# Nine fast product groups a layer instead of eight, and the residual parked in DRAM to make room

## The chip, the cores and the metric

The kernel runs on one core of a Trainium2 chip. The metric is device microseconds of one execution; times of runs are medians. The engines named below: TensorE (PE) multiplies, and PEld is its weight load; VectorE (DVE) and ScalarE (ACT) do the elementwise work; SyncE (SP) issues the DMAs; GpSimd (POOL) does nothing here.

## The reference

Two layers on x of 256 positions by 2048 features, all in float32. Layer 0 has a recurrent block (RG-LRU), layer 1 sliding-window attention with sinks; each ends with the same feed forward network, which is the part that the change touches.

```python
D_MODEL, SEQ, DEPTH = 2048, 256, 2
D_FF = 5632

def swiglu_ffn(x, g, w_in, w_out):
    h = rms_norm(x, g)
    gate, up = jnp.split(h @ w_in, 2, axis=-1)
    return x + (jax.nn.silu(gate) * up) @ w_out

for layer in range(DEPTH):
    if layer < N_REC:
        x = recurrent_block(x, ...)
    else:
        if layer == N_REC:
            k_band, v_band = shared_kv(x, kv_norm_g, w_kv, k_norm_g)
        x = attn_block(x, ..., k_band, v_band)
    x = swiglu_ffn(x, norm2_g[layer], ffn_w_in[layer], ffn_w_out[layer])
```

## The kernel before

**Layout.** Features lie on the 128 partitions, positions (T = 256) along the free dimension. The residual x is four tiles of 128 x 1024, each with four blocks of 128 features. Every weight is streamed once from DRAM, in jobs of 256 rows x 512 columns (512 KB, one DMA on SP's queue).

**Precision.** Each float32 operand is split into a high part `hi` (rounded to fp32r) and the rest `lo`, and a product is made of three matmuls: hi·hi, hi·lo and lo·hi. ACT makes `hi` (line 337), DVE subtracts to get `lo` (line 338).

**Jobs.** `stream` goes through a list of jobs. At job i it asks for the load of job i+4, splits the weights of job i+3, and emits the matmuls of job i. There are four buffers each of raw, hi and lo. Background work (generators) is emitted in between as far as a budget of DVE and ACT time allows (`DVE_TICK`, `ACT_TICK`, `DEBT`). That gives the order of the program. The framework then plans from it the order on each engine: an instruction whose inputs are ready in its model may go ahead of earlier ones that are not, and `issue_after` and `keep_in_program_order` restrain that.

**Feed forward input.** The 2 x 5632 columns are 22 groups of 512, each of eight jobs. A group yields 256 gate and 256 up features, and `silu(gate) * up` goes to a raw hidden tile.

- Groups 0 to 3 (`PLAIN`) start before the norm is known: they multiply x times the norm's gain, and their results are scaled by 1/rms afterwards (`start`). Meanwhile `normed` prepares the scaled and split input `xn`, and for six of the eight jobs also the mixed input `mx`.
- Of the others, groups 5, 7, ... 19 (`FAST`) are fast: in six of the eight jobs (`PAIRS`) the eight block products of a job are replaced by seven, in Strassen's way (Winograd's form), with mixed inputs and mixed weights. `mix` makes the mixed weights (lines 348 to 354: 349 to 351 build them in a tile d, 352 and 354 split them, 348 and 353 split the unmixed part). A job has then 21 matmuls instead of 24 (line 543). In the jobs 0 and 4 (`EVEN`) the mixed products come first. `joined` sums the product blocks into gate and up. The result stands with positions on the partitions, so that `turn` transposes it (line 738, four transposes), deferred until job 4 of the next fast group, or job 3 of the group after the last one.
- The remaining ones, 4, 6, ... 20 and 21, are plain groups on `xn` (`direct`). The one after the last fast group, 20, has some wide products: one matmul of 512 columns with the high and low part of x side by side in place of two of 256. `self.SYNC` puts such wide products into other groups of the program as well.
- After group 20, `split` is spawned: it splits the raw hidden tiles for the output product, each pair with one ACT copy and one DVE subtraction, which must come behind the last `mix` (`self.mark`).

**Feed forward output.** Four groups of 22 jobs; after each, `residual` adds the results into one tile of x.

**Memory.** Besides fixed buffers there are 33 work tiles of 128 x 1024 (`s0` to `s32`), handed out in the order in which they came free: five "near" ones, which `mix` and `joined` ask for, and 28 others. Between them lies a gap of 64 bytes. The four tiles of x are fixed and stand beside them.

Of the kernel before, what the change touches and what calls it, by code (L numbers as in the profile page):

```python
# [12 lines left out]
F32 = mybir.dt.float32  # L13
F32R = mybir.dt.float32r
AF = mybir.ActivationFunctionType
ALU = mybir.AluOpType

P = 128
D = 2048
T = 256  # L20
# [29 lines left out]
class Trunk:  # L50
# [10 lines left out]
    DEBT = 2500.0  # L61
    SYNC = (0, 1, 2)
    PLAIN = 4
    FAST = tuple(range(5, 20, 2))
    PAIRS = (0, 1, 2, 4, 5, 6)
    EVEN = (0, 4)
    OWED = 9000.0
    NEAR = 5
    MORE = 2800.0
    WARM = 30  # L70
    DVE_TICK = 640.0
# [2 lines left out]
    def __init__(self, ctx, tc, dram):  # L74
        self.tc, self.nc, self.d = tc, tc.nc, dram
        nc = self.nc
        const = ctx.enter_context(tc.tile_pool(name="const", bufs=1))
        psum = ctx.enter_context(tc.tile_pool(name="psum", bufs=1, space=bass.MemoryType.PSUM))
        self.par = const.tile([P, NPAR], F32, name="par")
        self.con = const.tile([P, NCON], F32, name="con")  # L80
        self.cc = const.tile([P, 32], F32, name="cc")
        self.rstd = [const.tile([P, T + 2], F32, name=f"rstd{i}") for i in range(2)]
        self.nm, self.nt = (const.tile([P, T + 2], F32, name=n) for n in ("nm", "nt"))
        self.r2 = const.tile([P, 2], F32, name="r2")
        self.rrs = [const.tile([P, 48], F32, name=f"rr{i}") for i in range(2)]
        self.zero = const.tile([P, P + T], F32R, name="zero")
        const.tile([P, PAD], F32, name="pad")
        self.x = [const.tile([P, 4, T], F32, name=f"x{i}") for i in range(4)]
        self.raw = [const.tile([P, 1024], F32, name=f"raw{i}") for i in range(4)]
        self.hi = [const.tile([P, 1024], F32R, name=f"hi{i}") for i in range(4)]  # L90
        self.lo = [const.tile([P, 1024], F32R, name=f"lo{i}") for i in range(4)]
        self.tmps = deque(const.tile([P, T], F32, name=f"t{i}") for i in range(4))
        self.halves = deque(const.tile([P, T], F32, name=f"h{i}") for i in range(4))
        self.sq = deque(const.tile([P, T], F32, name=f"sq{i}") for i in range(3))
        self.acc = self.sq.popleft()
        self.whole = [deque((i, 0) for i in range(self.NEAR, 33)), deque((i, 0) for i in range(self.NEAR))]
        self.stamp = 0
        self.keep = False
        self.part = {(d, n): deque() for d in (F32, F32R) for n in (False, True)}
        self.spool = const  # L100
        for i in range(33):
            if i == self.NEAR:
                const.tile([P, 16], F32, name="step")
            const.tile([P, 4 * T], F32, tag=f"s{i}", name=f"s{i}")
        self.held = {}
        self.sets = [[psum.tile([P, 512], F32, name=f"b{4 * i + j}") for j in range(4)] for i in range(2)]
        self.banks = deque(b for q in self.sets for b in q)
        self.misc = 0
        self.started = False
        self.jobs = []  # L110
        self.mixed = {}
        self.pend = deque()
        self.bg = deque()
        self.tick = -2 * self.LD
        self.dve = 0.0
        self.act = 0.0

# [45 lines left out]
    def double(self, dt=F32R, near=False):  # L163
        i, _ = self.pool(dt, near).popleft()
        s = self.spool.tile([P, 4 * T], dt, tag=f"s{i}", name=f"s{i}")
        self.held[id(s)] = (i, s)
        return s

    def back(self, i):
        self.whole[i < self.NEAR].append((i, self.stamp))  # L170
# [431 lines left out]
    def ffn(self, l, xs, r, gains, rn, col, out=None):  # L602
# [6 lines left out]
        two = lambda ap: ap.rearrange("p (a c) -> p a c", c=T)  # L609

        def normed():
# [3 lines left out]
            for p in range(8):  # L615
                while self.spare() < 4:
                    yield 1
                n, d = self.slot(F32), self.double()
# [5 lines left out]
                v = d[:, :].rearrange("p (a b c) -> p a b c", a=2, b=2)  # L624
# [6 lines left out]
                if p in self.PAIRS:  # L631
                    c, m = self.slot(F32), self.double()
# [11 lines left out]
                    self.free(c)  # L644
                    yield
                self.free(n)

        def split():
            for p in range(NH // 2):
# [19 lines left out]
        for g in range(NH // 2):  # L669
# [25 lines left out]
            def direct(ps, g=g):  # L695
# [14 lines left out]
                raw(g, s)  # L710
                if g == self.FAST[-1] + 1:
                    self.spawn(split())

            def joined(q, g=g):
                p1, c, u, h = self.half(), self.double(F32, True), self.slot(F32, True), self.slot(F32)
                twice = lambda ap: ap.unsqueeze(1).to_broadcast([P, 2, T])
                at = lambda i, n=1: q[i // 2][:, i % 2 * T:(i % 2 + n) * T]
                self.a(p1, at(5))
                self.tt(c[:, 3 * T:4 * T], at(4), p1, ALU.add)
                self.tt(two(u), two(at(6, 2)), twice(c[:, 3 * T:4 * T]), ALU.add)  # L720
                self.tt(c[:, 3 * T:4 * T], at(7), u[:, 0:T], ALU.add)
                self.tt(c[:, 0:T], at(3), p1, ALU.add)
                self.tt(c[:, T:2 * T], at(1), u[:, 0:T], ALU.add)
                self.tt(c[:, 2 * T:3 * T], at(2), u[:, T:2 * T], ALU.add)
                self.tt(c[:, 3 * T:4 * T], at(0), c[:, 3 * T:4 * T], ALU.add)
                for p in q:
                    self.free_bank(p)
                self.a(c[:, 0:2 * T], c[:, 0:2 * T], AF.Silu)
                self.tt(h, c[:, 2 * T:4 * T], c[:, 0:2 * T], ALU.mult)
                self.free_half(p1)  # L730
                self.free(c)
                self.free(u)

                def turn():
                    p = self.mbank()
                    for j in range(2):
                        for i in range(2):
                            nc.tensor.transpose(p[:, j * T + i * P:j * T + i * P + P],  # L738
                                                h[:, i * T + j * P:i * T + j * P + P],
                                                self.con[:, K_ID:K_ID + P])  # L740
                    s = self.slot(F32)
                    self.a(s, p)
                    self.free_mbank(p)
                    self.free(h)
                    raw(g, s)
                self.pend.append(turn)
# [4 lines left out]
            elif g in self.FAST:  # L751
                self.fast_group(src, xn, mx, g, joined, g == self.FAST[-1])
            else:
                end = g == self.FAST[-1] + 1
                self.group(src, ND, xn, direct, g == NH // 2 - 1, (0, 3, 4, 5) if end else (), True, 3 if end else None)
            if g == 0:
                def begin():
                    self.spawn(normed())
                    self.DEBT = self.OWED
                    self.keep = True  # L760
                self.jobs[-8] = self.with_(self.jobs[-8], begin)
        n = len(self.jobs)
        self.project(self.d[f"ffn_out{l}"], NH, hid, gains, rn, out)

        def end():
            self.DEBT = Trunk.DEBT
            self.keep = False
        self.jobs[n] = self.with_(self.jobs[n], end)

    def with_(self, job, first):  # L770
        src, mm, fast = job
# [600 lines left out]
```

## Time and profile before

| | us |
|---|---|
| median of 3 runs | 1979.45 (1979.3 to 1979.98) |
| profiled execution | 1980.0 |
| its span, first to last instruction | 1978.2 |
| PE busy | 1969.5, 16576 matmuls |
| PEld busy | 1927.9 |
| DVE busy | 1489.9 |
| ACT busy | 1123.8 |

In layer 1, group 0 of the feed forward input starts at about 1266 us of the span, group 4 at 1355.2, the first fast group at 1377.0, and the output product at 1735.6; layer 0 has the same stages some 970 us earlier.

Times in the profile's rows are microseconds from the start of the span, durations of one instruction are nanoseconds where "mean ns" stands. Matmuls overlap in the pipeline: one lasts 276 ns, but the next starts 113 ns after it, so PE's work is read from the distance of starts, or from the chain of waits, which lists the time that each piece added. A row of a timeline is start, duration, engine, line and operation, output<-inputs, shapes, count, and in brackets the idle time ahead of it with what ended it.

### The profile page before, as it was taken

The page shows a single profiled execution, that of the slowest core. Times are in us where ns is not written, and L with a number is a line of the kernel's source. Part 1 is how long each engine was busy: PE and PEld are TensorE (multiplying, and loading weights), DVE is VectorE, ACT ScalarE, POOL GpSimd, SP SyncE. Part 2 cuts the span into 40 slices and gives each one's busy share as a digit, 9 for nine tenths or more (in the row PEclk, how much of TensorE's full clock was granted, in tenths as well). Part 3 has the DMA queues.
Part 4 walks back from the last instruction along what each step waited for, and adds up shares of the span by engine and source line. Part 5 has one row for each costly group of instructions (what it writes and reads, how often), then busy time and mean ns, then how long its engine had stood idle before and what let it go on. Part 6 is the DMA issues. An engine that isn't in the chain of part 4 may idle for free. (4 is left out here: it accounts for less than half of the span.)

```text
span 1978.2 us, 40228 instructions
## 1 busy us (share of the span) xinstructions
PE 1969.5 (100%) x16576; PEld 1927.9 (97%) x16576; DVE 1489.9 (75%) x2375; ACT 1123.8 (57%) x1642; POOL 0.2 (0%) x4
## 2 busy tenths in 40 slices
PE   9999999999999999999999999999999999999999
PEld 9999999999999999999998789999999999999999
DVE  8989868788888896554667776697888888844443
ACT  7798756555555565444556775564555555644442
POOL 0000000000000000000000000000000000000000
PEclk9999999999999999999999999999999999999999
DMA  7555655555566556556554334555666565656663
GB/s 274 189 190 180 202 195 181 197 199 196 193 207 208 199 193 202 193 191 199 195 182 145 122 118 151 191 189 185 200 209 209 193 201 196 205 196 204 204 204 128
DMA packets 105016, 376.57 MB, mean 190 GB/s; under 512 B 11648, under 2 KB 13824, under 8 KB 104832
## 3 DMA queue, kind: packets, MB, share of 16 engines
q1 hardware_dynamic: 104544, 373.60, 57.1%
q8 instruction: 129, 2.11, 0.4%
q14 instruction: 55, 0.45, 0.1%
q10 hardware_dynamic: 288, 0.40, 0.1%
HBM read 371.86 MB, written 2.10 MB: 189 GB/s over the span
## 5 line engine op out<-in xcount | busy, mean ns | idle before, releaser
L385 PE MATMUL b<-s,hi 128*128 128x256 f32 (+1 forms) x8190 | 1093.4, 280 | 2.0 <-ACT s L127 1.3
L385 PEld LDWEIGHTS b<-s,hi 128*128 128x128 f32 x8190 | 1017.8, 188 | 15.2 <-ACT s L127 2.2
L338 DVE TENSOR_TENSOR lo<-raw,hi 128x1024 fp32r<-128x1024 f32 (+1 forms) x609 | 740.7, 1220 | 374.2 <-ACT hi L337 371.3
L337 ACT ACTIVATE hi<-raw 128x1024 fp32r<-128x1024 f32 (+1 forms) x609 | 641.0, 1056 | 524.4 <-PE b L385 430.9
L385 PE MATMUL b<-s,lo 128*128 128x256 f32 x4224 | 626.7, 276 | 0.0
L385 PEld LDWEIGHTS b<-s,lo 128*128 128x128 f32 x4224 | 547.3, 188 | 0.2
L352 ACT ACTIVATE s<-s 128x1024 fp32r<-128x1024 f32 x96 | 102.1, 1063 | 169.9 <-DVE s L351 169.9
L543 PE MATMUL b<-hi,s 128*128 128x256 f32 x1088 | 180.5, 277 | 0.0
L543 PEld LDWEIGHTS b<-hi,s 128*128 128x128 f32 x1088 | 154.7, 188 | 0.0
L543 PE MATMUL b<-s,s 128*128 128x256 f32 x1152 | 149.7, 279 | 0.0
L543 PEld LDWEIGHTS b<-s,s 128*128 128x128 f32 x1152 | 139.8, 189 | 0.0
L354 DVE TENSOR_TENSOR s<-s,s 128x1024 fp32r<-128x1024 f32 x96 | 117.6, 1225 | 27.6 <-ACT s L352 27.6
L543 PE MATMUL b<-lo,s 128*128 128x256 f32 x544 | 129.5, 276 | 0.0
L127 ACT ACTIVATE s<-s 128x512 fp32r<-128x512 f32 (+3 forms) x174 | 85.2, 521 | 30.9 <-DVE s L136 23.9
L543 PEld LDWEIGHTS b<-lo,s 128*128 128x128 f32 x544 | 92.6, 188 | 0.0
L353 DVE TENSOR_TENSOR lo<-raw,hi 128x768 fp32r<-128x768 f32 x96 | 91.3, 951 | 0.0
L348 ACT ACTIVATE hi<-raw 128x768 fp32r<-128x768 f32 x96 | 78.7, 841 | 21.2 <-issue 11.7
L349 DVE TENSOR_TENSOR s<-raw 128x512 f32<-128x512 f32 x96 | 66.1, 689 | 24.2 <-DMA raw<-in_ffn_in 23.1
L1262 PE MATMUL b<-hi,s 128*128 128x512 f32 x256 | 83.4, 406 | 0.0
L136 DVE TENSOR_TENSOR s<-s,s 128x512 fp32r<-128x512 f32 (+2 forms) x143 | 74.6, 551 | 4.9 <-ACT s L127 4.7
L127 ACT ACTIVATE s<-b 128x256 fp32r<-128x256 f32 (+4 forms) x114 | 51.0, 481 | 24.6 <-PE b L1236 6.7
L1262 PEld LDWEIGHTS b<-hi,s 128*128 128x128 f32 x256 | 45.8, 188 | 9.6 <-issue 1.2
(118 smaller groups left out, 1105.9 us busy)
## 6 DMA issues: line engine op xcount, KB each, us to landing
raw<-in_ffn_in SPq DMA_DIRECT2D x352, 512.0 KB, 3.7
raw<-in_ffn_out SPq DMA_DIRECT2D x176, 512.0 KB, 3.9
raw<-in_lru_in SPq DMA_DIRECT2D x63, 512.0 KB, 4.0
raw<-in_lru_out SPq DMA_DIRECT2D x32, 512.0 KB, 3.4
raw<-in_w_q SPq DMA_DIRECT2D x32, 512.0 KB, 3.2
raw<-in_w_o SPq DMA_DIRECT2D x32, 512.0 KB, 3.3
raw<-in_gate SPq DMA_DIRECT2D x8, 512.0 KB, 4.1
raw<-in_kv SPq DMA_DIRECT2D x8, 512.0 KB, 3.3
```

The lines of the kernel that those rows point to most:

```text
L127: self.nc.scalar.activation(out, in_, func, **kw)
L136: self.nc.vector.tensor_tensor(out, a, b, op)
L337: self.nc.scalar.activation(hi[:, q], raw[:, q], AF.Copy)
L338: self.nc.vector.tensor_tensor(lo[:, q], raw[:, q], hi[:, q].bitcast(F32), ALU.subtract)
L348: act(hi[:, q], raw[:, q], AF.Copy)
L349: tt(two(d[:, 0:2 * T]), two(raw[:, T:3 * T]), raw[:, 0:T].unsqueeze(1).to_broadcast([P, 2, T]), ALU.subtract)
L352: act(mh[:, :], d[:, :], AF.Copy)
L353: tt(lo[:, q], raw[:, q], hi[:, q].bitcast(F32), ALU.subtract)
L354: self.mark = tt(ml[:, :], d[:, :], mh[:, :].bitcast(F32), ALU.subtract)
L385: self.nc.tensor.matmul(ps[f][:, 0:c1 - c0], w, x2[k][:, c0:c1], start=f not in begun, stop=last and all(q[1] != f for q in todo[n + 1:]))
L543: nc.tensor.matmul(st["ps"][b][:, h % 2 * T:(h % 2 + n) * T], x, w, start=b not in st["begun"], stop=True, skip_group_check=True)
L1262: nc.tensor.matmul(st[g][b][:, :], x, q, start=c + kt == 0 and x is xh and q is wh, stop=c == 7 and kt == 1 and q is wl)
```

## The change

In each layer's feed forward input the fast groups are 4, 6, ... 20: nine instead of eight, the first straight behind group 3. The plain group with the wide products and the spawn of `split` is then 21, the last one. To have work tiles for it, x becomes four tiles of the work pool, which has 37 now, seven of them near. As soon as `normed` has read a tile of x, `park` stores it to DRAM and frees it; in the output product `fetch` loads the four back, in the jobs 2, 7, 12 and 17 (the first 22 jobs end with the first use). `joined` sums with fewer, wider operations (512 columns where two of 256 stood next to each other), which leaves gate and up interleaved in another order, so that `turn` reads the halves the other way round, and it no longer uses near tiles. During the stage the budget per half job for DVE is 780 ns instead of 640 (740 in layer 1).

```diff
--- before.py
+++ after.py
@@ -61,11 +61,13 @@
     DEBT = 2500.0
     SYNC = (0, 1, 2)
     PLAIN = 4
-    FAST = tuple(range(5, 20, 2))
+    FAST = tuple(range(4, 21, 2))
     PAIRS = (0, 1, 2, 4, 5, 6)
     EVEN = (0, 4)
     OWED = 9000.0
-    NEAR = 5
+    BUSY = 780.0
+    WORK = 37
+    NEAR = 7
     MORE = 2800.0
     WARM = 30
     DVE_TICK = 640.0
@@ -85,7 +87,6 @@
         self.rrs = [const.tile([P, 48], F32, name=f"rr{i}") for i in range(2)]
         self.zero = const.tile([P, P + T], F32R, name="zero")
         const.tile([P, PAD], F32, name="pad")
-        self.x = [const.tile([P, 4, T], F32, name=f"x{i}") for i in range(4)]
         self.raw = [const.tile([P, 1024], F32, name=f"raw{i}") for i in range(4)]
         self.hi = [const.tile([P, 1024], F32R, name=f"hi{i}") for i in range(4)]
         self.lo = [const.tile([P, 1024], F32R, name=f"lo{i}") for i in range(4)]
@@ -93,16 +94,22 @@
         self.halves = deque(const.tile([P, T], F32, name=f"h{i}") for i in range(4))
         self.sq = deque(const.tile([P, T], F32, name=f"sq{i}") for i in range(3))
         self.acc = self.sq.popleft()
-        self.whole = [deque((i, 0) for i in range(self.NEAR, 33)), deque((i, 0) for i in range(self.NEAR))]
+        self.whole = [deque((i, 0) for i in range(self.NEAR, self.WORK)), deque((i, 0) for i in range(self.NEAR))]
         self.stamp = 0
+        self.tick = -2 * self.LD
         self.keep = False
         self.part = {(d, n): deque() for d in (F32, F32R) for n in (False, True)}
         self.spool = const
-        for i in range(33):
+        for i in range(self.WORK):
             if i == self.NEAR:
                 const.tile([P, 16], F32, name="step")
             const.tile([P, 4 * T], F32, tag=f"s{i}", name=f"s{i}")
         self.held = {}
+        self.x, self.xt = [None] * 4, [None] * 4
+        for i in range(4):
+            self.place(i)
+        self.dram = ctx.enter_context(tc.tile_pool(name="dram", bufs=1, space=bass.MemoryType.DRAM))
+        self.away = {}
         self.sets = [[psum.tile([P, 512], F32, name=f"b{4 * i + j}") for j in range(4)] for i in range(2)]
         self.banks = deque(b for q in self.sets for b in q)
         self.misc = 0
@@ -111,7 +118,6 @@
         self.mixed = {}
         self.pend = deque()
         self.bg = deque()
-        self.tick = -2 * self.LD
         self.dve = 0.0
         self.act = 0.0
 
@@ -165,6 +171,22 @@
         s = self.spool.tile([P, 4 * T], dt, tag=f"s{i}", name=f"s{i}")
         self.held[id(s)] = (i, s)
         return s
+
+    def place(self, i):
+
+        n, _ = self.whole[0].pop() if self.tick < 0 else self.whole[1].popleft()
+        s = self.spool.tile([P, 4 * T], F32, tag=f"s{n}", name=f"s{n}")
+        self.held[id(s)] = (n, s)
+        self.xt[i], self.x[i] = s, s[:, :].rearrange("p (f t) -> p f t", t=T)
+
+    def park(self, i):
+        self.away[i] = self.dram.tile([P, 4 * T], F32, name=f"away{self.tick}_{i}")
+        self.nc.sync.dma_start(self.away[i][:, :], self.xt[i][:, :])
+        self.free(self.xt[i])
+
+    def fetch(self, i):
+        self.place(i)
+        self.nc.sync.dma_start(self.xt[i][:, :], self.away[i][:, :])
 
     def back(self, i):
         self.whole[i < self.NEAR].append((i, self.stamp))
@@ -644,6 +666,8 @@
                     self.free(c)
                     yield
                 self.free(n)
+                if p % 2:
+                    self.park(p // 2)
 
         def split():
             for p in range(NH // 2):
@@ -712,22 +736,21 @@
                     self.spawn(split())
 
             def joined(q, g=g):
-                p1, c, u, h = self.half(), self.double(F32, True), self.slot(F32, True), self.slot(F32)
+                c, u, h = self.double(F32), self.double(F32), self.slot(F32)
                 twice = lambda ap: ap.unsqueeze(1).to_broadcast([P, 2, T])
                 at = lambda i, n=1: q[i // 2][:, i % 2 * T:(i % 2 + n) * T]
-                self.a(p1, at(5))
-                self.tt(c[:, 3 * T:4 * T], at(4), p1, ALU.add)
-                self.tt(two(u), two(at(6, 2)), twice(c[:, 3 * T:4 * T]), ALU.add)
-                self.tt(c[:, 3 * T:4 * T], at(7), u[:, 0:T], ALU.add)
-                self.tt(c[:, 0:T], at(3), p1, ALU.add)
-                self.tt(c[:, T:2 * T], at(1), u[:, 0:T], ALU.add)
-                self.tt(c[:, 2 * T:3 * T], at(2), u[:, T:2 * T], ALU.add)
-                self.tt(c[:, 3 * T:4 * T], at(0), c[:, 3 * T:4 * T], ALU.add)
+                part = lambda i, n=1: u[:, i * T:(i + n) * T]
+                self.a(part(3), at(5))
+                self.tt(part(0), at(4), part(3), ALU.add)
+                self.tt(two(part(1, 2)), two(at(6, 2)), twice(part(0)), ALU.add)
+                self.tt(part(0), at(7), part(1), ALU.add)
+                self.tt(c[:, 0:2 * T], at(0, 2), part(0, 2), ALU.add)
+                self.tt(c[:, 2 * T:4 * T], at(2, 2), part(2, 2), ALU.add)
                 for p in q:
                     self.free_bank(p)
-                self.a(c[:, 0:2 * T], c[:, 0:2 * T], AF.Silu)
-                self.tt(h, c[:, 2 * T:4 * T], c[:, 0:2 * T], ALU.mult)
-                self.free_half(p1)
+                v = c[:, :].rearrange("p (a b c) -> p a b c", a=2, b=2)
+                self.a(v[:, :, 1, :], v[:, :, 1, :], AF.Silu)
+                self.tt(two(h), v[:, :, 0, :], v[:, :, 1, :], ALU.mult)
                 self.free(c)
                 self.free(u)
 
@@ -736,7 +759,7 @@
                     for j in range(2):
                         for i in range(2):
                             nc.tensor.transpose(p[:, j * T + i * P:j * T + i * P + P],
-                                                h[:, i * T + j * P:i * T + j * P + P],
+                                                h[:, (1 - i) * T + j * P:(1 - i) * T + j * P + P],
                                                 self.con[:, K_ID:K_ID + P])
                     s = self.slot(F32)
                     self.a(s, p)
@@ -757,6 +780,7 @@
                 def begin():
                     self.spawn(normed())
                     self.DEBT = self.OWED
+                    self.usual, self.DVE_TICK = self.DVE_TICK, self.BUSY
                     self.keep = True
                 self.jobs[-8] = self.with_(self.jobs[-8], begin)
         n = len(self.jobs)
@@ -764,8 +788,11 @@
 
         def end():
             self.DEBT = Trunk.DEBT
+            self.DVE_TICK = self.usual
             self.keep = False
         self.jobs[n] = self.with_(self.jobs[n], end)
+        for i in range(4):
+            self.jobs[n + 2 + 5 * i] = self.with_(self.jobs[n + 2 + 5 * i], lambda i=i: self.fetch(i))
 
     def with_(self, job, first):
         src, mm, fast = job
```

## The prediction

> **What bounds the kernel now.** I read the page's busy shares first, then the chain of waits around the changed stage, then the timelines of VectorE (DVE), TensorE (PE) and ScalarE (ACT) where the first fast group of layer 1 starts.
>
> ```profile
> span 1978.2 us, 40228 instructions
> PE 1969.5 (100%) x16576; PEld 1927.9 (97%) x16576; DVE 1489.9 (75%) x2375; ACT 1123.8 (57%) x1642; POOL 0.2 (0%) x4
> 1376.99 19.90 PE b L543 x174
> 1396.89 21.76 PE b L385 x192
> 1418.65 9.96 PE b L543 x87
> 1428.61 0.44 PE b L738 x4
> 1429.05 9.96 PE b L543 x87
> ```
>
> PE is busy in all but 8.7 us of the span, so the time is the sum of PE's steps. The chain (start, duration, what) gives their prices. A plain group is 192 matmuls in 21.76 us, 113.3 ns each. A fast group is 174 matmuls (six jobs of 21, two of 24) in 2 x 9.96 = 19.92 us. The turn of an earlier fast group's result, four transposes, is a further 0.44 us, which the first fast group of a layer doesn't have.
>
> **The sum.** Each layer exchanges one plain group for a fast one: groups 5, 7 ... 19 become 4, 6 ... 20. Away go 21.76 us, in come 19.92 + 0.44 = 20.36 us: 1.40 us a layer, 2.80 us in both. The group with wide products after the last fast one moves from 20 to 21 with its matmuls unchanged: price nothing.
>
> [...]
>
> **What must stay hidden: six more mixed jobs a layer on DVE and ACT.** Groups of instructions (count, busy, mean ns):
>
> ```profile
> L338 DVE TENSOR_TENSOR lo<-raw,hi 128x1024 fp32r<-128x1024 f32 (+1 forms) x609 | 740.7, 1220 | 374.2 <-ACT hi L337 371.3
> L349 DVE TENSOR_TENSOR s<-raw 128x512 f32<-128x512 f32 x96 | 66.1, 689 | 24.2 <-DMA raw<-in_ffn_in 23.1
> L350 DVE TENSOR_TENSOR s<-raw,s 128x256 f32<-128x256 f32 x96 | 40.4, 420 | 1.1
> L351 DVE TENSOR_TENSOR s<-raw,s 128x256 f32<-128x256 f32 x96 | 40.7, 424 | 2.7
> L353 DVE TENSOR_TENSOR lo<-raw,hi 128x768 fp32r<-128x768 f32 x96 | 91.3, 951 | 0.0
> L354 DVE TENSOR_TENSOR s<-s,s 128x1024 fp32r<-128x1024 f32 x96 | 117.6, 1225 | 27.6 <-ACT s L352 27.6
> 1333.50:1355.20 21.70, 21.70 (x185) 21.35 (x184) 12.74 (x18) 9.86 (x13) 0.00 (x0) 1.00 0.61 202
> 1355.20:1377.00 21.80, 21.80 (x195) 21.80 (x194) 18.53 (x26) 11.30 (x13) 0.00 (x0) 1.00 0.55 191
> ```
>
> A mixed job costs DVE 689 + 420 + 424 + 951 + 1225 = 3709 ns against 1220 for a plain one: 2.49 more, 14.9 us a layer. PE takes 19.92 / 174 x 21 = 2.40 us for the job, so DVE must run ahead into the plain group before. The last two rows are groups 3 and 4 of layer 1 (length, then PE, PEld, DVE, ACT busy). Group 3 leaves DVE 21.7 - 12.7 = 9.0 us idle, and that is the cover: three of the new mixes (7.5 us) go there, as three go into group 4 now. ACT is busy for half of both groups and pays under 1 us a job.
>
> How near the edge is it? The last mixed job of a fast group is the tightest. DVE's timeline, then PE's:
>
> ```profile
> 1379.05 1.23 DVE L354 TENSOR_TENSOR s<-s,s 128x1024 fp32r<-128x1024 f32 x1 [1.13 <-ACT s L352]
> 1386.22 1.23 DVE L354 TENSOR_TENSOR s<-s,s 128x1024 fp32r<-128x1024 f32 x1 [0.26 <-ACT s L352]
> 1390.22 1.23 DVE L354 TENSOR_TENSOR s<-s,s 128x1024 fp32r<-128x1024 f32 x1
> 1392.65 1.52 PE L543 MATMUL b<-s,s 128*128 128x256 f32 x12
> ```
>
> DVE delivers job 6's mixed tile at 1390.22 + 1.23 = 1391.45, and PE turns to the mixed products at 1392.65: 1.2 us to spare. In the new place the same stretch also holds group 3's closing sums, which a group of the first kind (results not yet scaled by the norm) needs and group 4 doesn't:
>
> ```profile
> 1353.88 0.42 DVE L136 TENSOR_TENSOR h<-b,t 128x256 f32<-128x256 f32 x1
> ...
> 1355.67 0.42 DVE L136 TENSOR_TENSOR h<-b,rstd 128x256 f32<-128x256 f32 x1
> ```
>
> Six operations, 1353.88 to 1356.09, some 2.1 us. DVE's idle gaps of 1.13 and 0.26 us (bracketed above) can take 1.4 of it. Left are 0.7 us against 1.2 to spare, so I take no wait. The other end, no gap used: 2.1 - 1.2 = 0.9 us of PE waiting a layer. Nothing can be gained there.
>
> A wait has an after-price. PE has two paces at the same granted clock of 1.00:
>
> ```profile
> 1283.02 1.10 PE L385 MATMUL b<-s,lo 128*128 128x256 f32 x8
> 1285.85 1.10 PE L385 MATMUL b<-s,lo 128*128 128x256 f32 x8
> 1294.28 1.07 PE L385 MATMUL b<-s,lo 128*128 128x256 f32 x8
> 1428.45 0.60 PE L738 MATMUL b<-con,s 128*128 128x128 f32 x4
> 1428.80 1.68 PE L543 MATMUL b<-s,s 128*128 128x256 f32 x12
> 1432.38 1.52 PE L543 MATMUL b<-s,s 128*128 128x256 f32 x12
> ```
>
> From the first row to the second, 24 matmuls, are 2.83 us: 118 ns each against the 113.3 of a plain group; the eight last of a job show as 1.10 or 1.07 us. The slow pace follows an interruption (here the norm's matmuls) and stays until wide products, or the first job of a fast half, restore it: after the turn at 1428.45 twelve matmuls take 1.68 us, at 1432.38 1.52 again. A wait in group 4's job 6 would thus cost 4.6 ns on some 216 matmuls up to group 6, 1.0 us.
>
> **The joined sums.** Six operations of 256 columns and two of 512 become two and four:
>
> ```profile
> 1692.53 0.68 DVE L136 TENSOR_TENSOR s<-b,s 128x512 f32<-128x512 f32 x1
> 1693.46 1.40 DVE L136 TENSOR_TENSOR s<-b,s 128x256 f32<-128x256 f32 x4
> ```
>
> Four narrow ones take 1.40 us in a row, two wide ones at most 2 x 0.68 = 1.36: DVE gains next to nothing after each fast group and loses nothing, off the path or on it. The new turn reads the halves in the other order, the same four transposes.
>
> **Park and fetch.** Each layer adds four stores and four loads of 512 KB on SP's queue, 8.4 MB for both layers.
>
> ```profile
> raw<-in_ffn_in SPq DMA_DIRECT2D x352, 512.0 KB, 3.7
> x<-in_x SPq DMA_DIRECT2D x3, 512.0 KB, 7.2
> SPq L323 <- DVE lo L338: 1070.7, 451, 6.6
> ACT hi L337 <- PE b L385: 430.9, 300, 2.6
> L140 DVE SCALAR_TENSOR_TENSOR s<-x,par,rstd x32: 467/474/484, 326.0 to 1325.9; 128x256 f32<-128x256 f32 x32
> 1794.27 0.75 DVE L136 TENSOR_TENSOR x<-x,b 128x256 f32<-128x256 f32 x2
> ```
>
> A park waits for DVE's last scaled read of its four columns; behind it on SP stand weight loads, and those wait for DVE too (the SPq row), so a park holds back little that wasn't held. In layer 1 all reads of x are over by 1325.9, before the first new mix. ACT's row shows the splits waiting for PE to release buffers, not for loads: a load late by a job (2.72 us) stays hidden. The fetches are asked for in output jobs 2, 7, 12 and 17; the residual's first use is at 1794.27, after 22 jobs, so the last has 5 jobs, 13.6 us, against 7.2 us to land. Price nothing; the other end is four fetches in one row ahead of a weight load. At four times the 3.7 us that one load takes that is at most 14.8 us, less the three to four jobs (8 to 11 us) by which loads run ahead: 4 to 7 us a layer. The fast groups already wait for loads now and then (the 23.1 us in L349's row), but fetches can't start before the near tiles come free, at the end of the last fast group, ahead of plain work; nearest is nothing.
>
> **Splitting the hidden tiles.** It is now spawned after group 21, the last one. But the instructions' order per engine is planned from readiness, not from the place of the call. Now it is spawned at group 20's end, 1713.9, and runs far earlier:
>
> ```profile
> 1675.42 0.63 ACT L127 ACTIVATE s<-s 128x512 fp32r<-128x512 f32 x1
> 1684.50 1.23 DVE L354 TENSOR_TENSOR s<-s,s 128x1024 fp32r<-128x1024 f32 x1
> 1685.64 1.29 DVE L136 TENSOR_TENSOR s<-s,s 128x512 fp32r<-128x512 f32 x2
> ```
>
> DVE starts right behind the last mix (L354), 28 us ahead of the spawn. One group later the same distance holds, so a dozen pairs are ready when the output starts, which uses one a job. Price nothing, and nothing to gain, as PE doesn't wait here now; unhidden, one ACT copy and one DVE subtraction, 0.63 + 0.65 = 1.3 us of PE waiting a layer.
>
> **Total.** 1980.0 us for the profiled execution (its span 1978.2 and 1.8 around it) - 2.8 = 1977.2. The median shown, 1979.45, lies 0.55 below the profiled one: 1976.6.
>
> **Rivals.**
> 1. The mixes for group 4 come late. For: 0.5 us of margin. Against: idle gaps, and seven near tiles instead of five. 0.9 + 1.0 us in each layer: 1976.6 + 3.8 = 1980.4.
> 2. Slower: that wait leaves PE in the slow pace for the rest of the stage. Groups 5 to 20 have no wide products: 8 x 192 + 8 x 174 = 2928 matmuls at 4.6 ns are 13.5 us a layer. It decides once the delay passes the 0.5 us; one layer gives 1976.6 + 0.9 + 13.5 = 1991, both 2005. Against: the rows from 1428.45 on, where a fast half restores the pace.
> 3. The fetches bunch ahead of weight loads: at the lower end, 4 us in one layer, 1980.6; the cover above speaks against it.
> 4. All four stages are planned anew, since tiles are handed out in another order, and some of PE's 8.7 us of idle time goes: about 2 us less, 1974.6. That the exchange itself fails isn't possible: the matmuls are counted.
>
> **How the numbers follow.** About 0.2%, 4 us, is what a measurement of this kernel can tell from no change. Forecast 0.62 (1975.6 to 1978), rival 1 0.15, rival 2 0.07, rival 3 0.06, rival 4 0.10. Faster by over 0.2% (below 1975.5): rival 4 and a little of the forecast, 0.16. Slower (above 1983.4): rival 2, and rivals 1 and 3 at worse than their prices, 0.14. The range from 1974.6 to 1982.0 leaves out rival 2 and those tails.
>
> **What would show it.** Right: nine fast groups in the chain of each layer, the first at group 4, at 19.9 us each; no PE wait on L352 or L354; x8 rows of 1.07 in group 5; the first split before group 21 ends; the span about 2.8 us shorter. Wrong: a PE gap at the first fast group's last mixed job, 1.10 rows behind it, PE waiting at the first output job, or DMA waits of ACT or DVE in group 21.

## The result, and the profile after

| | before | after |
|---|---|---|
| median of 20 runs, us | 1980.06 (1979.09 to 1981.21) | 1976.76 (1976.15 to 1977.4) |
| span of the profiled execution, us | 1978.2 | 1975.1 |
| matmuls | 16576 | 16548 |
| PE idle in the span, us | 8.7 | 8.3 |

The ratio is 0.9983, 95% interval 0.9977 to 0.9989: 3.3 us, 0.17%, clear of no change. 1976.6 was forecast.

The head of the page after:

```profile
span 1975.1 us, 40195 instructions
PE 1966.8 (100%) x16548; PEld 1925.4 (97%) x16548; DVE 1514.6 (77%) x2399; ACT 1131.8 (57%) x1656; POOL 0.2 (0%) x4
```

PE's busy time fell by 2.7 us. DVE's rose by 24.7 without becoming the limit. The 28 matmuls less are 2 x (18 - 4): each layer saves 18 in the exchanged group and adds four transposes.

The chain of waits after, where layer 1's fast groups begin and where the last one ends (start, duration, engine, line; L565 is the fast groups' matmul, L407 the plain one, L761 the turn):

```profile
1353.59 19.90 PE b L565 x174
1373.48 21.76 PE b L407 x192
1395.25 9.96 PE b L565 x87
1405.20 0.44 PE b L761 x4
...
1718.97 253.06 PE b L407 x2196
```

The first fast group stands where plain group 4 stood, at the price of the others, and the chain runs on in PE alone. PE's waits in the whole of the program after:

```profile
PE b L1326 <- DVE zero L1323: 1.3, 1, 1.3
PE b L407 <- ACT s L133: 1.2, 2, 0.8
PE b L1185 <- DVE s L151: 1.1, 4, 0.5
PE b L1140 <- ACT s L133: 0.9, 1, 0.9
...
```

The two others are of 0.3 us each, for ACT's L359 and L133. None names the mixing lines (L371 to L376) or a load.

### The profile page after: what moved, and what is told of

Read it like the earlier page. It is cut to its first block, busy times and chain, and to the rows that moved or that the text cites. A ratio compares the mean times of both kernels' runs of the same rounds, so it can differ in the third digit from the quotient of the medians.

```text
span 1975.1 us, 40195 instructions
## 1 busy us (share of the span) xinstructions
PE 1966.8 (100%) x16548; PEld 1925.4 (97%) x16548; DVE 1514.6 (77%) x2399; ACT 1131.8 (57%) x1656; POOL 0.2 (0%) x4
## 5 line engine op out<-in xcount | busy, mean ns | idle before, releaser
L407 PE MATMUL b<-s,hi 128*128 128x256 f32 (+1 forms) x7934 | 1060.1, 281 | 1.6 <-ACT s L133 1.2
L407 PEld LDWEIGHTS b<-s,hi 128*128 128x128 f32 x7934 | 986.5, 188 | 14.7 <-ACT s L133 2.2
L359 ACT ACTIVATE hi<-raw 128x1024 fp32r<-128x1024 f32 (+1 forms) x597 | 628.3, 1056 | 502.3 <-PE b L407 400.9
L407 PE MATMUL b<-s,lo 128*128 128x256 f32 x4096 | 607.3, 277 | 0.0
L407 PEld LDWEIGHTS b<-s,lo 128*128 128x128 f32 x4096 | 530.4, 188 | 0.2
L565 PE MATMUL b<-hi,s 128*128 128x256 f32 x1224 | 203.2, 277 | 0.0
L565 PEld LDWEIGHTS b<-hi,s 128*128 128x128 f32 x1224 | 174.1, 188 | 0.0
L565 PE MATMUL b<-s,s 128*128 128x256 f32 x1296 | 168.4, 279 | 0.0
L565 PEld LDWEIGHTS b<-s,s 128*128 128x128 f32 x1296 | 157.2, 189 | 0.0
L376 DVE TENSOR_TENSOR s<-s,s 128x1024 fp32r<-128x1024 f32 x108 | 132.0, 1223 | 23.6 <-ACT s L374 23.6
L565 PE MATMUL b<-lo,s 128*128 128x256 f32 x612 | 145.8, 277 | 0.0
L565 PEld LDWEIGHTS b<-lo,s 128*128 128x128 f32 x612 | 104.2, 188 | 0.0
L133 ACT ACTIVATE s<-s 128x512 fp32r<-128x512 f32 (+3 forms) x174 | 86.1, 523 | 30.4 <-DVE s L142 18.5
L371 DVE TENSOR_TENSOR s<-raw 128x512 f32<-128x512 f32 x108 | 74.3, 688 | 22.0 <-DMA raw<-in_ffn_in 21.6
L133 ACT ACTIVATE s<-b 128x256 fp32r<-128x256 f32 (+4 forms) x134 | 58.8, 468 | 24.9 <-PE b L1263 6.8
L142 DVE TENSOR_TENSOR s<-b,s 128x512 f32<-128x512 f32 (+3 forms) x126 | 63.4, 533 | 5.3 <-ACT s L133 3.9
```

The source lines that it names most:

```text
L133: self.nc.scalar.activation(out, in_, func, **kw)
L142: self.nc.vector.tensor_tensor(out, a, b, op)
L359: self.nc.scalar.activation(hi[:, q], raw[:, q], AF.Copy)
L371: tt(two(d[:, 0:2 * T]), two(raw[:, T:3 * T]), raw[:, 0:T].unsqueeze(1).to_broadcast([P, 2, T]), ALU.subtract)
L376: self.mark = tt(ml[:, :], d[:, :], mh[:, :].bitcast(F32), ALU.subtract)
L407: self.nc.tensor.matmul(ps[f][:, 0:c1 - c0], w, x2[k][:, c0:c1], start=f not in begun, stop=last and all(q[1] != f for q in todo[n + 1:]))
```

## The experiments

Spans are compared with 1975.1 after and 1978.2 before; ratios are to the kernel before, run on the same chip. Line numbers shift by a few between kernels.

### The exchange and the rest, each alone

All of the change but the ninth group:

```diff
-    FAST = tuple(range(4, 21, 2))
+    FAST = tuple(range(5, 20, 2))
```

> The changed kernel with the fast groups put back to 5, 7 ... 19: parked residual, 37 tiles, wider sums and the larger DVE budget stay. Exchange theory (each plain group exchanged for a fast one is worth 1.40 us and nothing else in the change matters): PE's 28 matmuls come back, the span grows by 2.8 us to 1977.9, about 0.3 us below the kernel before, a ratio near 0.9998. Relief theory (part of the gain comes from the shorter sums, the additional near tiles or the budget): it stays 1 us or more closer to the changed kernel, below 1977.

Measured: 1980.11 us, ratio 0.9998 (0.9989 to 1.0007), span 1978.3, 16576 matmuls. With eight fast groups the parking, the two additional near tiles, the wide sums and the budget are together worth nothing, and the theory that they relieve something there falls. Subtracting this kernel from the one after gives the exchange by stage: layer 1's key and value products start at 1006.3 here and at 1004.8 after (1.5 us), the last norm's matmuls at 1279.0 and 1277.2 (1.8), the end comes at 1978.3 and 1975.1 (3.2). So the two feed forward stages give 1.5 and 1.4 us, and 0.3 arises between them.

The other way round, the kernel before with the ninth group and nothing else:

```diff
-    FAST = tuple(range(5, 20, 2))
+    FAST = tuple(range(4, 21, 2))
```

> The kernel before with the fast groups moved to 4, 6 ... 20 and nothing else: x fixed, 33 tiles, five near, old sums, old budget. Exchange theory: the same 2.8 us of gain, span near 1975.4. Memory theory (the ninth group needs the tiles that x lends): instructions wait for tiles, PE stands still at group 4 or late in the stage, and the gain is gone or turned round: span 1978 or more, with PE waits on L352 or L354 that neither kernel has.

Measured: 1979.26 us, ratio 0.9994 (0.9985 to 1.0003), span 1978.7. The median lies 1.3 us below the kernel before, which can't be told from no change; the whole change gains 3.3. The profiled execution, with 1980.44 us, is the second slowest of its eleven, so that it shows where the gain can be lost, and not what is lost on the average. Layer 1 does what it does after: from the first fast group at 1357.19 to the end are 621.5 us, as from 1353.59 to 1975.1. Layer 0 loses 3.8 us against the kernel after. Some of it is a wait; PE's timeline of this kernel, job 6 of layer 0's first fast group:

```profile
402.69 0.97 PE L543 MATMUL b<-s,s 128*128 128x256 f32 x6 [0.53 <-ACT s L352]
...
405.00 0.95 PE L543 MATMUL b<-s,s 128*128 128x256 f32 x6 [1.12 <-DVE s L354]
```

This is rival 1, the late mix, in one layer, with 1.65 us; PE's list of waits has it together with a later one of 0.2 us, at 615.6:

```profile
PE b L543 <- DVE s L354: 1.3, 2, 1.1
...
PE b L543 <- ACT s L352: 0.5, 1, 0.5
```

DVE's timeline shows why the mix is late:

```profile
401.46 2.35 DVE L338 TENSOR_TENSOR lo<-raw,hi 128x1024 fp32r<-128x1024 f32 x2
403.73 1.22 DVE L354 TENSOR_TENSOR s<-s,s 128x1024 fp32r<-128x1024 f32 x1
```

Two plain subtractions stand straight ahead of job 6's last mix. In the kernel after this mix begins at 399.27, and the plain subtractions follow it, four in a row from 400.42. So the change as a whole has another order planned for DVE. Most of what else layer 0 loses, 1.5 us, lies between 609 and 652 us, where one plain group runs at the slow pace behind the wait of 0.2 us. Of the change's parts, the wide sums, the budget and the parking were each taken out of the kernel after below, and none of those brought the wait back. The seven near tiles weren't tried alone, nor two parts together: which of them makes the better order stays open.

### Parking taken out

x keeps four of the 37 work tiles; no store, no load back:

```diff
-                if p % 2:
-                    self.park(p // 2)
...
-            self.jobs[n + 2 + 5 * i] = self.with_(..., lambda i=i: self.fetch(i))
+            pass
```

> The changed kernel without park and fetch: x keeps its four of the 37 work tiles all the time, so 33 are left; nine fast groups, wider sums and the larger budget stay. Exchange theory: same as the changed kernel within 0.5 us (span 1974.6 to 1975.6), since the eight stores and eight loads were hidden. Memory theory: short of tiles, slower than the changed kernel by 2 us or more, the waits lying in the fast groups.

Measured: 1985.93 us, ratio 1.0027 (1.0017 to 1.0037), span 1984.0, 8.9 us over the kernel after. PE has no new wait, so tiles aren't short. The chain of waits of layer 1:

```profile
1353.53 20.10 PE b L565 x174
1373.62 22.61 PE b L407 x192
1396.24 9.95 PE b L565 x87
...
1406.63 10.15 PE b L565 x87
```

Up to 1353.53 the kernel is level with the one after. Then every plain group takes 22.61 us, 117.8 ns a matmul, and every second half of a fast group 10.15; first halves keep their 9.95. That is the slow pace of the prediction, at granted clock 1.00 and with no wait to start it. It begins inside a job; PE's timeline, job 6 of a fast group:

```profile
1409.96 1.52 PE L565 MATMUL b<-s,s 128*128 128x256 f32 x12
...
1412.36 1.59 PE L565 MATMUL b<-s,s 128*128 128x256 f32 x12
```

Twelve mixed products took 1.52 us in job 5 and take 1.59 in job 6. Followed through the program's hand-out of tiles, job 6's mixed input (`mx`) lies in a near tile here in layer 1 alone; in layer 0, and in both layers before and after, all mixed inputs lie in far tiles, on the other side of the 64 byte gap. So the theory became: parking is worth 8.9 us, for where it puts one tile. The kernel before with the ninth group has no parking either, but its own hand-out; there all mixed inputs lie far, and layer 1's plain groups take 21.76 us.

### The same placement by hand

Everything of the kernel after, but job 6's mixed input in a near tile:

```diff
-                    c, m = self.slot(F32), self.double()
+                    c, m = self.slot(F32), self.double(near=p == 6)
```

> The changed kernel with one allocation moved: the mixed input of job 6 (mx[6]) is asked from the near tiles in both layers. In the kernel without parking exactly that tile lay in a near one, in layer 1 alone, and there PE fell to the slow pace at job 6 of every fast group without any wait. Placement theory: the same here in both layers, 0.2 us in each second half of a fast group and 0.85 us in each plain group behind one, about 9 us a layer, 18 us slower than the changed kernel (1994), no PE wait on any engine. Rival, shortage theory (that kernel was slow because DVE or the DMAs were late for want of tiles, and the tile was an accident): within 1 us of the changed kernel.

Measured: 1994.64 us, ratio 1.0070 (1.0055 to 1.0085), span 1992.9, 17.8 us over the kernel after, where the placement theory gave 18. No wait is new. Its chain of waits:

```profile
1362.46 20.09 PE b L565 x174
1382.55 22.61 PE b L407 x192
...
1415.56 10.15 PE b L565 x87
```

The same prices as without parking, now in both layers: layer 0 had already lost 8.9 us when this stretch began (1362.46 against 1353.59). Parking, fetches and their DMAs were all there, so the placement makes the slow pace and not their absence.

Then the kernel without parking again, with the 64 bytes moved ahead of the near tiles, so that near and far tiles adjoin:

```diff
-            if i == self.NEAR:
+            if i == 0:
                 const.tile([P, 16], F32, name="step")
```

> The kernel without park and fetch (1985.9 before), with the gap of 64 bytes laid ahead of the near tiles instead of behind them, so that near and far tiles have the same place within 4 KB. Placement theory, refined: what matters is the 64 bytes between near tiles and the others, so mx[6] in a near tile does no harm any more and the plain groups of layer 1 are back at 21.76 us; but now the mixed weights of the jobs 1, 2, 5 and 6 lie as far tiles do, and if the near place is needed for them, the fast jobs lose the pace instead, in both layers. Shortage theory: unchanged, 22.6 us per plain group in layer 1.

Measured: 1982.57 us, ratio 1.0010 (1.0001 to 1.0020), span 1980.8, 3.2 less than with the gap in its place. Its chain of waits:

```profile
1356.39 20.22 PE b L565 x174
1376.61 21.76 PE b L407 x192
1398.37 10.12 PE b L565 x87
```

Both prices have changed places: plain groups are back at 21.76, and every fast half takes 10.12 in place of 9.96. 18 halves x 0.16 = 2.9 us a layer, 5.8 in both, against 5.7 measured over the kernel after; the first such stage had lost its share by 1356.39 (2.8 us behind 1353.59). Against the kernel without parking nothing differs but that the near tiles lie 64 bytes further on, against the far ones and against all fixed buffers. These 64 bytes decide the pace here: the plain groups go from 22.61 to 21.76 us and the fast halves from 9.96 to 10.12. Layer 1's job 6 has its mixed input and its mixed weights in near tiles in either kernel, at an unchanged distance from each other, so that this pair alone can't be what slows the plain groups: what differs for it is where it lies against the far tiles and the fixed buffers. Which operands have to stand how, no run singles out.

### The order of the jobs 0 and 4

The prediction said that the first job of a fast half restores the pace. In the jobs 0 and 4 the mixed products come first; here this is undone:

```diff
-            if c in self.EVEN:
-                todo = todo[3:] + todo[:3]
```

> The changed kernel with the products of the jobs 0 and 4 of a fast group in the same order as in the other jobs (unmixed first); the placement of all tiles and the number of products are unchanged. Order theory (the mixed products coming first restore PE's pace after an interruption): the slow pace that follows each turn is no longer ended before group 21, some 2900 matmuls at 4.6 ns a layer, up to 13 us a layer or 26 in all, about 2003. Placement theory (the far mixed weights of these two jobs restore it wherever they come in the job): a few matmuls later back to pace, under 0.2 us a half, at most 3 us in all.

Measured: 1977.84 us, ratio 0.9986 (0.9976 to 0.9996), span 1976.1. Its chain of waits:

```profile
1395.78 9.99 PE b L565 x87
...
1406.21 9.97 PE b L565 x87
1416.18 21.76 PE b L407 x192
```

The plain groups keep 21.76 us: the order within the job doesn't restore the pace. What does stays open. The jobs 0 and 4 have their mixed weights in far tiles, the other mixed jobs in near ones, as the expectation says; that fits, but wasn't changed. Halves take 0.01 to 0.04 us longer, and this is the 1.0 us by which the span is longer, half of it in each layer (from layer 0's first fast group to the key and value products 619.0 us, 618.5 after; from layer 1's to the end 622.0, 621.5 after).

The recurrent block, which this edit doesn't touch, shows something about the slow pace. All tiles lie where they lie in the kernel after, and the same group follows a wait of about 0.75 us for ACT in both. PE's timeline here, then after:

```profile
161.33 1.07 PE L407 MATMUL b<-s,lo 128*128 128x256 f32 x8
```

```profile
161.41 1.10 PE L407 MATMUL b<-s,lo 128*128 128x256 f32 x8
```

One has the fast pace to its end and the other the slow one. The time so won isn't kept: PE comes early to the next products and waits 0.80 us for ACT's L133 at 188, a wait that the kernel after doesn't have, and by 207 us both are level.

### A late mix made on purpose

In the ninth group's job 6 the last subtraction of `mix` is done four times, 3.4 us more of DVE:

```diff
         tt(ml[:, :], d[:, :], mh[:, :].bitcast(F32), ALU.subtract)
+        if i in self.late4:
+            for _ in range(3):
+                tt(ml[:, :], d[:, :], mh[:, :].bitcast(F32), ALU.subtract)
```

> The changed kernel with DVE made late once a layer: in group 4, job 6, the subtraction that ends the mix is done four times instead of once, 3 x 1.14 = 3.4 us more on DVE. The prediction's price of a late mix: 3.4 us less the 1.5 us that the changed kernel has to spare there is a PE wait of about 1.9 us on that instruction, then the slow pace up to group 6's first job, 216 matmuls at 4.6 ns or 1.0 us: 2.9 us a layer, 5.8 in all. Rival (slow pace to the end of the stage): 15 us a layer. Rival (order planned anew around the longer work): no wait, under 1 us.

One execution: 1982.99 us, span 1981.2, 6.1 over the kernel after. PE's waits and, below them, the chain of waits of layer 1 (line numbers are three higher than after):

```profile
PE b L568 <- DVE s L379: 4.8, 2, 3.0
```

```profile
1376.59 2.39 PE b L568 x18
1378.98 22.38 PE b L410 x190
1401.36 9.96 PE b L568 x87
...
1421.71 21.76 PE b L410 x192
```

The late tile costs 1.8 us of waiting in this layer and then one slow plain group: 190 matmuls in 22.38 us against 21.53 at 113.3 ns, 0.85 us. The next fast half has its 9.96, and from there on the pace is normal. In layer 0 the wait is longer, and yet no slow group follows; PE's timeline:

```profile
407.21 0.96 PE L568 MATMUL b<-s,s 128*128 128x256 f32 x6 [2.96 <-DVE s L379]
...
410.95 1.07 PE L410 MATMUL b<-s,lo 128*128 128x256 f32 x8
```

The 4.8 us of waits, one slow group and about 0.5 us on the 18 matmuls behind the waits, in both layers together, make the 6.1. The forecast of 5.8 came near with both terms off: the waits were longer than twice 1.9 us, and the after-price fell due once and not twice. Rival 2, the slow pace to the end of the stage after a wait, falls.

### Parts that move nothing, and two that ask for more

The narrow sums and the old order of the transposes back in:

```diff
-                self.tt(c[:, 0:2 * T], at(0, 2), part(0, 2), ALU.add)
-                self.tt(c[:, 2 * T:4 * T], at(2, 2), part(2, 2), ALU.add)
+                self.tt(c[:, 0:T], at(3), p1, ALU.add)
+                ...
+                self.tt(c[:, 3 * T:4 * T], at(0), c[:, 3 * T:4 * T], ALU.add)
```

> The changed kernel with the old joined sums (six operations of 256 columns and two of 512, two near tiles taken for them) and the old order of the transposes. Exchange theory: same as the changed kernel within 0.5 us, since DVE has idle time behind each fast group. Relief theory: the sums hold back the next group's weight splits, DVE is 0.1 to 0.3 us later after each of 18 fast groups, and up to 3 us of the gain go.

Measured: 1976.85 us, ratio 0.9981 (0.9971 to 0.9990), span 1974.7. The wide sums are worth nothing that can be told.

The larger DVE budget taken out:

```diff
-                    self.usual, self.DVE_TICK = self.DVE_TICK, self.BUSY
+                    self.usual = self.DVE_TICK
```

> The changed kernel with the old background budget for DVE (640 and 740 ns per half job instead of 780 during the feed forward input). Exchange theory: only the order of the program moves, and each engine's order is planned from readiness, so the time stays within 0.7 us of the changed kernel. Rival: the scaled and mixed inputs are not ready for group 4, PE waits there on L376 or on a mixed input, 1 to 4 us a layer.

Measured: 1976.66 us, ratio 0.9983 (0.9974 to 0.9992), span 1976.4. Nothing either.

A seventh mixed job in every fast group:

```diff
-    PAIRS = (0, 1, 2, 4, 5, 6)
+    PAIRS = (0, 1, 2, 3, 4, 5, 6)
```

> The changed kernel with seven mixed jobs in a fast group instead of six (job 3 too). PE has 3 matmuls less in each of 18 groups, 54 x 113.3 ns = 6.1 us, and if DVE could hide it, the span would be 1969. Reckoned for DVE: 7 x 3.71 + 1.22 + 3.2 (sums) + 9.8 + 0.7 = 40.9 us in a pair of groups that PE then does in 41.8, and 1.3 us behind in each mixed job while a lead of 8 us is all that the buffers allow. So I expect PE to wait for the mixes in every fast group, 2 to 4 us each, and the kernel to be 25 to 60 us slower. That tells how near nine groups of six are to DVE's limit.

Measured: 2027.96 us, ratio 1.0235 (1.0219 to 1.0251), span 2027.8. PE's waits say why:

```profile
PE b L565 <- DVE s L376: 26.2, 36, 0.9
PE b L565 <- ACT s L374: 11.0, 26, 1.0
```

36 times PE waits for the last subtraction of a mix, and 26 times for ACT's copy just before it. So the mixing does run out of DVE a short way above six jobs in every second group. That the plain group before is the cover that the ninth group lives on is argued from its idle time, not tested. PE waits in all eighteen fast groups here, and of the sixteen plain groups between them a single one then runs at the slow pace, all its rows of eight at 1.10 us from 1584.94 on; the others have 1.07.

The last one tries to use the pace: wide products, behind which it came back in the kernel after (wide at 1287.97, then a row of eight of 1.10 us at 1289.85 and of 1.07 from 1292.63 on), in two more early groups.

```diff
-            self.group(..., sync=self.SYNC if g == 2 else ())
+            self.group(..., sync=self.SYNC if g in (1, 2) else ())
...
-            self.group(..., g == 3, self.SYNC if g % 2 else ())
+            self.group(..., g == 3, self.SYNC if g else ())
```

> The changed kernel with wide products in two more groups of the recurrent block (x group 1 and y group 2, which have none and run at the slow pace, 1.10 us rows, for their whole length and into the next group). Pace theory: each job back at 113.3 instead of 118 ns a matmul saves 0.11 us; about 4 jobs of x group 1 and one of x group 2, 5 jobs of y group 2, 48 gate matmuls and 2 to 3 jobs of y group 3: 1.2 to 1.6 us less than the changed kernel, span near 1973.7. Rival (the pace there is set by something else, waits or loads): the rows stay at 1.10 and the time within 0.5 us, or longer by the additional sums of eight wide results (eight ACT copies and DVE sums).

Measured: 1976.92 us, ratio 0.9983 (0.9975 to 0.9992), span 1976.3: no gain. PE's timeline shows the pace coming back in one of the groups, rows of eight matmuls:

```profile
163.70 1.10 PE L407 MATMUL b<-s,lo 128*128 128x256 f32 x8
166.48 1.07 PE L407 MATMUL b<-s,lo 128*128 128x256 f32 x8
```

From the third job on the rows are 1.07, where the kernel after stays at 1.10 in this group. Whether the wide products did it can't be told from one group, since the kernel with the old order of the jobs has 1.07 there without them. What the group gains isn't kept: this kernel comes to it 0.30 us ahead of the one after (154.88 against 155.18), PE then comes early to the next products and waits 0.76 us for ACT's L133 at 187.75, and behind that it is 0.28 us ahead (189.90 against 190.18). So the faster rows buy nothing there: the wait for ACT takes what they gain. In layer 0's feed forward this execution then loses 1.4 us, 0.9 of it in waits for DVE's `lo` at fast groups; it is the slowest of its eleven, 1.2 us over their median.

## Why the prediction was right, point by point

- **The sum.** Forecast 1.40 us a layer, measured 1.5 and 1.4. The turn cost its 0.44 us (1405.20 to 1405.64), though a single transpose lasts 272 ns in the trace after: four times that, 1.1 us a turn, would have left about 1.5 us in the two stages, and not 2.9. The 2.80 of the sum stand against 3.1 in the span; the 0.3 lies outside the two stages. That 1976.6 came within 0.2 us of the median is luck in part: it starts from a median of 1979.45, and the 20 runs of the kernel before gave 1980.06, from which the same sum gives 1977.3.
- **Planning anew (rival 4)** happened in small. Between before and after, single groups of layer 0's recurrent block changed their pace: in the group around 190 to 208 us all rows of eight matmuls took 1.10 us before. PE's timeline after has 1.07 from the third job on:

```profile
193.00 1.10 PE L407 MATMUL b<-s,lo 128*128 128x256 f32 x8
195.78 1.07 PE L407 MATMUL b<-s,lo 128*128 128x256 f32 x8
```

  This is worth about 0.6 us; the groups ahead of it start 0.3 us later than before (161.41 against 161.13). Such shifts have both signs, and what is left of them fits the 0.3. The 2 us that the rival priced didn't come: PE's idle time fell by 0.4.
- **The margin of the late mix** was forecast at 0.5 us and is 1.5. DVE's timeline before, then DVE's and PE's after:

```profile
1389.01 1.22 DVE L338 TENSOR_TENSOR lo<-raw,hi 128x1024 fp32r<-128x1024 f32 x1
```


```profile
1354.43 0.42 DVE L142 TENSOR_TENSOR h<-b,t 128x256 f32<-128x256 f32 x1
...
1356.43 0.42 DVE L142 TENSOR_TENSOR h<-b,rstd 128x256 f32<-128x256 f32 x1
...
1366.55 1.23 DVE L376 TENSOR_TENSOR s<-s,s 128x1024 fp32r<-128x1024 f32 x1 [0.46 <-ACT s L374]
1367.69 4.63 DVE L360 TENSOR_TENSOR lo<-raw,hi 128x1024 fp32r<-128x1024 f32 x4
```

```profile
1369.24 1.52 PE L565 MATMUL b<-s,s 128*128 128x256 f32 x12
```

  Job 6's mix is ready at 1366.55 + 1.23 = 1367.78, PE turns to it at 1369.24. The six closing sums came in between, as forecast; but before, a plain subtraction of 1.22 us stood straight ahead of this last mix, and after, none stands between the last two mixes, and four (4.63 us) follow the last. The one that went behind is about the 1.0 us by which the margin is larger. The term that was off is the order of the other work on DVE, which the prediction took as fixed. That rival 1 didn't come is owed to this order: with another one, in the kernel before with the ninth group, PE waited at this place in layer 0.
- **Splits** started where forecast, right behind the last mix, and were further along than "a dozen": 20 of the 22 by the end of group 21. DVE's timeline, then the group of these instructions between 1702 and 1732.6:

```profile
1701.04 1.22 DVE L376 TENSOR_TENSOR s<-s,s 128x1024 fp32r<-128x1024 f32 x1 [1.12 <-ACT s L374]
1702.19 1.28 DVE L142 TENSOR_TENSOR s<-s,s 128x512 fp32r<-128x512 f32 x2
```

```profile
L142 DVE TENSOR_TENSOR s<-s,s 128x512 fp32r<-128x512 f32 x20 | 13.2, 690 | 0.0
```

- **Park and fetch** cost nothing, as forecast, but the park step named the wrong wait. It said that a park waits for DVE's last scaled read of the tile. In the trace the last store waits for the last write, the residual's sum, and not for that read. DVE's last sum, then the rows of the parked tile (DMA issues, ns, first and last start in us):

```profile
1265.18 0.42 DVE L142 TENSOR_TENSOR s<-s,b 128x256 f32<-128x256 f32 x1
```


```profile
L184 SPq DMA_DIRECT2D away<-s x8: 326/326/424, 233.2 to 1265.6; - x8
L189 SPq DMA_DIRECT2D s<-away x8: 422/424/490, 733.2 to 1711.4; - x8
```

  The sum ends at 1265.60 and the last store starts at 1265.6, while the norm's last scaled read starts only at 1324.5. The loads back are asked for at 1700 to 1711, in the second half of the last fast group, earlier than the output jobs in which they stand, and land in 6.7 us in the middle.

- **What parking is for** was the step that was incomplete. The prediction had it only as DMAs to be hidden and priced them at nothing. Taken out of this kernel it costs 8.9 us, since the tiles are then handed out so that job 6's mixed input of layer 1 becomes a near one. The forecast came out because the change as made happens to keep all mixed inputs far. Nothing in the prediction provides for that: here it was luck.
- **The slow pace.** "Follows an interruption" is right only now and then. Of twenty plain groups that follow a fast group with a wait (two in the kernel before with the ninth group, two in the one with the late mix, sixteen in the one with seven mixed jobs) three ran at the slow pace, so the 1.0 us that the prediction sets behind a wait is seldom due. "Stays until wide products, or the first job of a fast half" is mostly right in time: in the kernel after the rows are 1.07 us from 1292.63 on, behind the wide products at 1287.97, and without parking the fast halves behind slow plain groups take 9.95 us; but in the kernel before the group at 187.77 us has wide products and keeps 1.10 to its end. It isn't that the mixed products stand first in a fast half, and an interruption isn't needed: where the operands lie can start the slow pace, as in the plain groups of 22.61 us without parking. Rival 2's 13.5 us a layer had the right kind of price under the wrong condition: 8.9 us a layer arise from placement, none of it from a wait.

## What to carry to other kernels

Where one engine is busy 99.6% of the span, count its instructions and price them by the chain of waits; here that gave the change to half a microsecond. Then ask what else a part of the change moves: a part whose own work is hidden can still decide where buffers lie, so compare the duration of equal pieces of the chain (21.76 against 22.61), not waits alone. And test the parts singly in both directions: the rest without the ninth group was worth nothing, the ninth group without the rest nothing that could be told from no change, and both together gave 3.2 us in the span.

## What the runs showed of the hardware that was not expected

PE showed two paces for the same 128x256 matmul at granted clock 1.00: 113.3 and 117.8 ns (21.76 and 22.61 us for 192). Which one held depended on where the operands lay: one mixed input of each layer in a near tile instead of a far one cost 17.8 us over the two layers, and 64 bytes of gap moved the loss from plain groups (0.85 us each) to fast halves (0.16 us each). The pace outlasted the matmuls that started it: plain groups, which don't use the tile, took 22.61 us each, and the fast half behind them had its 9.95 us again. But the place isn't all: behind the same wait of about 0.75 us and with all tiles in the same places, one group had rows of 1.10 us in one kernel and of 1.07 in another. Each kernel has one trace, so how often a group falls to either side from one execution to the next isn't shown. What inside PE or the memory makes the slow pace, no run here shows.
